# A hybrid gating/state-space layer on one core: mixing in halves, later root transposes, stores on ScalarE's queue, shared border splits, finer side pieces, residual sums in a row

## The chip, the cores and the metric

The kernel runs on one core of a Trainium2 chip. The metric is the device time of one execution in microseconds (us); for several runs, their median. Engines: TensorE (PE), VectorE (DVE), ScalarE (ACT), GpSimd (POOL) and SyncE (SP), which computes nothing here and issues DMAs.

## The reference

One layer over 2048 tokens of width 1024, all in float32. Cut to what is computed:

```python
hc = _rms(ctx) * norm1_w * (1 + csc1) + csh1        # 256 context tokens: only their final scan states are used
_, st_f, st_b = _token_mixer(hc, zero_state, zero_state, ...)
hl = _rms(x) * norm1_w * (1 + sc1) + sh1            # shifts, scales and gates from silu(c) @ w_ada
# _token_mixer(hl, st_f, st_b):
proj = h @ w_in                                     # u, v (1024 each), z (1024), xBC (1536), dt (32)
xbc = silu(conv_centred(xBC))                       # 5 taps
y = ssd_forward + ssd_backward                      # chunks of 128, 16 heads of 64, state 128, 2 groups
g = (y + xs * d_skip) * silu(z)
ssd_out = _rms(g in 2 groups of 512) * ssd_norm_w
u, v = gelu(u), _rms(gelu(v) in 8 heads of 128) * gm_norm_w
mixed = einsum('hts,bcshd->bcthd', gm_ws, v) + gm_bs   # 128 x 128 per head and chunk
x = x + g1 * (concat[u * mixed, ssd_out] @ w_out)
hl = _rms(x) * norm2_w * (1 + sc2) + sh2
x = x + g2 * ((silu(hl @ w_gate) * (hl @ w_up)) @ w2)  # hidden width 2816
return _rms(x) * final_norm_w
```

## The kernel before

Tokens are worked in two blocks of 1024 (blk 1 first, then 0), each in two halves of 512 (TB); a chunk is 128 tokens (P). Every float32 operand of a large product is split in a high and a low part (`hi`, `lo`), and a product of 128 x 128 by 512 columns is done as three (`mm3`, L234 to L236; L1142 to L1144 and L1271 to L1273 in the FFN). ScalarE casts the high part and VectorE subtracts for the low one (`split`, L1026 to L1028; `wlo`, L221, for projection weights). A block of 24 such products fills one of PSUM's banks: 3 are called `mmp`, 5 `smp`.

The stages in order: projection, convolution and transposes of xBC of block 1; `proj_v`, `proj_u`, `proj_z` of block 1 beside context scans and the backward scan; xBC of block 0; then the long stretch of some 800 us in which `run` advances a main chain (`proj_z(0)`, `proj_v(0)`, `proj_u(0)` and three quarters of the output projection, `out_half`) and a side chain in turn: the rest of the backward scan (`ssd_bwd`) and then `ssd_y`, 2.61 side steps (`SIDE`) to each block of main. Then the last quarter of `out_half` with `border`, which prepares the FFN; `ffn1(0)`, `ffn2(0)` (with `prep_1`, the preparation of block 1, as its side), `ffn1(1)`, `ffn2(1)`. The FFN works with seven products of sums for eight (tiles of such sums are made by L1031 and L1034).

`proj_v(blk)`: for two groups of four heads (hh) and two token halves (j), four chunks c: a block of 24 products, gelu (`gelu2`, L588 to L592: square, product, tanh, product), squares for the norm. `mixing(hh, j, vh)` does the four heads' 128 x 128 products (L631) for the j before, when c is 2: for each head it loads weights and biases `gw` (L627, L628; two buffers), multiplies, and adds on VectorE (L633). The last j's mixing stands at the end of `proj_v`. `proj_u` loads the mixed rows (L612) and multiplies them with its gelu.

`ssd_y` walks 32 items (chunk c, group g): `y_load` loads the item's record; `y_seg` (item ahead) loads per half of the heads (q) the factor rows fb and bb from `fscr` (L751, L752), broadcast over all partitions, and makes the masked decay matrices from them (L757 on ScalarE, L758 to L760, L761, product on GpSimd L762); `y_out` does the item's products (L776 to L787), and VectorE's sums (L782 to L798); `y_store` transposes the item's result (L806), copies it and stores it (L809). After every eighth item `y_rstd` computes the reciprocal roots of the group norm with `newton` (L242 to L247: a chain of small VectorE instructions), transposes them (L819), copies and stores them (L822, `r3scr`). Main and side share the pools `tma` (14 buffers), `xin` (8) and `sml`.

What sets the order: the program's calls fix a data flow, and a scheduler that the framework runs ahead of time places the instructions; on the chip each engine takes its own in that fixed order, and an instruction that waits holds all behind it. All DMAs, loads and stores, are issued by SyncE in one such order. In `to_tok` (L471) transposed rows of xBC are stored the same way.

In the FFN, `hl_split` (L1097) splits four tiles of sums, `slow(prep_1(), 2, 10)` puts a piece of the side (four in all) after every ten steps of `ffn2`, `upd` (L1252) adds a finished down product to the residual, `sq_acc` (square on ScalarE L261, add L264) sums its squares, and `final` (L1291: a product with ones, root, L1295 scale, L1296 store) ends a half.

Of the kernel before, what the change touches and what calls it, by code (L numbers as in the profile page):

```python
# [14 lines left out]
P = 128  # L15
# [68 lines left out]
def kernel(ctx: ExitStack, tc: tile.TileContext, xT, ctxp, cc, crow, wad1, wad2, vecs, rows,  # L84
# [378 lines left out]
    def to_tok(o, n, q, ch):  # L463
# [7 lines left out]
        DMA.dma_start(rec[q][g][:, :, coff:coff + P].rearrange("c p x -> p c x"),  # L471
# [132 lines left out]

    def proj_u(blk, hs):
        for h0 in range(0, 8, 2):
            us = [unit(U_U + h0), unit(U_U + h0 + 1)]
            for j in range(2):
                ts_ = slice((blk * 2 + j) * TB, (blk * 2 + j + 1) * TB)
                for i, (hi, lo) in enumerate(us):  # L610
# [4 lines left out]
                    flush()  # L615
                    t = gelu2(ps, tmp)
# [4 lines left out]
    def proj_v(blk, hs):  # L621
        def mixing(hh, j, vh):
            ts_ = slice((blk * 2 + j) * TB, (blk * 2 + j + 1) * TB)
            for h in range(4):
# [3 lines left out]
                DMA.dma_start(gw[:, 1, :], gmb[:, hd * P:(hd + 1) * P].broadcast_to([P, P]))  # L628
                ps = smp()
# [9 lines left out]
        for hh in range(2):  # L639
            us = [unit(U_V + hh * 4 + i) for i in range(4)]  # L640
            for j in range(2):
                vh = []
                ms = sml()[:, :16]
                for c in range(4):
# [8 lines left out]
                    if c == 2 and prev is not None:  # L653
                        mixing(*prev)
# [9 lines left out]
        mixing(*prev)  # L664
# [72 lines left out]

    def y_load(pools, i, c, g):
        return {"rc": load_rec(pools[i % 3 == 2], c, g, True)}

    def y_seg(st, c, g):
# [5 lines left out]
        for q in range(2):  # L747
            h0 = g * 8 + q * 4
            fb, bb = tma()[:, :TB], tma()[:, :TB]
            o = ((c % 4) * 32 + h0) * P  # L750
            DMA.dma_start(fb, fscr[c // 4][:, o:o + TB].broadcast_to([P, TB]))  # L751
            DMA.dma_start(bb, fscr[c // 4][:, o + 16 * P:o + 16 * P + TB].broadcast_to([P, TB]))  # L752
# [50 lines left out]
    def y_store(ya, c, g):  # L803
# [5 lines left out]
        DMA.dma_start(sscr[c // 4][g * TB:(g + 1) * TB, (c % 4) * P:(c % 4 + 1) * P].rearrange("(i p) t -> p i t", p=P),  # L809
# [3 lines left out]
    def y_rstd(tb, ms):  # L813

        V.tensor_scalar(out=ms, in0=ms, scalar1=1.0 / TB, scalar2=4 * EPS, op0=ALU.mult, op1=ALU.add)
        r = newton(ms, 8)
        yield
        ps = smp()
        PE.transpose(out=ps[0:8, :P], in_=r, identity=ident)  # L819
        t = tma()  # L820
        S.copy(t[0:8, :P], ps[0:8, :P])
        DMA.dma_start(r3scr[tb].rearrange("g (c x) -> (g c) x", x=P), t[0:8, :P])  # L822

    def ssd_y(rp):
        its = [(c, g) for c in range(NCH) for g in range(2)]
        st = {}
        st[0] = y_load(rp, 0, *its[0])
        yield from y_seg(st[0], *its[0])
        st[1] = y_load(rp, 1, *its[1])
        store = None  # L830
        for i, (c, g) in enumerate(its):
# [6 lines left out]
            y = yield from y_out(st.pop(i), c, g, ms[:, g * 4 + c % 4:g * 4 + c % 4 + 1])  # L838
            if store is not None:
                yield from y_store(*store)  # L840
            store = (y, c, g)
            if g == 1 and c % 4 == 3:
                yield from y_rstd(c // 4, ms)
        yield from y_store(*store)

# [574 lines left out]
```

## Time and profile before

| what | value |
|---|---|
| runs shown | 2985.91, 2975.28, 2970.30 us (median 2975.28) |
| the profiled execution's own time | 2980.2 us |
| its span, first to last instruction | 2978.4 us |
| mean granted TensorE clock | 0.971 |
| busy: PE, DVE, ACT, POOL | 95%, 66%, 43%, 21% |
| TensorE in the stretch 800 to 1550 us | busy 684.97 of 750, clock 0.95 |

The profile is of one execution. It is read in this order: the busy shares tell which engine has no room; the waits of that engine tell what its gaps are for, each named by its line and by what ended the gap; a timeline of the engine that was late tells why. The granted clock is read beside them, since TensorE works the same product in 0.23 us or 0.43 us by it.

### The profile page before, as it was taken

The page shows a single profiled execution, that of the slowest core. Times are in us where ns is not written, and L with a number is a line of the kernel's source. Part 1 is how long each engine was busy: PE and PEld are TensorE (multiplying, and loading weights), DVE is VectorE, ACT ScalarE, POOL GpSimd, SP SyncE. Part 2 cuts the span into 40 slices and gives each one's busy share as a digit, 9 for nine tenths or more (in the row PEclk, how much of TensorE's full clock was granted, in tenths as well). Part 3 has the DMA queues.
Part 4 walks back from the last instruction along what each step waited for, and adds up shares of the span by engine and source line. Part 5 has one row for each costly group of instructions (what it writes and reads, how often), then busy time and mean ns, then how long its engine had stood idle before and what let it go on. Part 6 is the DMA issues. An engine that isn't in the chain of part 4 may idle for free. (4 is left out here: it accounts for less than half of the span.)

```text
span 2978.4 us, 36719 instructions
## 1 busy us (share of the span) xinstructions
PE 2815.9 (95%) x12478; PEld 2252.8 (76%) x12478; DVE 1977.8 (66%) x3012; ACT 1272.8 (43%) x2360; POOL 637.6 (21%) x550
## 2 busy tenths in 40 slices
PE   7999989999998898998979899999999899999997
PEld 2788778788677676776768688888778788888885
DVE  6776866886678788777876655556766544445555
ACT  4445343344356455443543533333544333333443
POOL 3100000101132232322302344444210322221000
PEclk8999999999999999998989899999999999999998
DMA  6222567742755588786758444445766333334664
GB/s 223 91 88 89 178 217 236 247 135 85 229 178 147 173 248 250 221 257 214 245 164 278 165 152 163 159 151 181 253 218 204 127 106 106 106 100 132 227 192 155
DMA packets 296744, 528.03 MB, mean 177 GB/s; under 512 B 28998, under 2 KB 89830, under 8 KB 296556
## 3 DMA queue, kind: packets, MB, share of 16 engines
q1 hardware_dynamic: 296556, 525.69, 55.3%
q8 instruction: 98, 1.61, 0.2%
q14 instruction: 90, 0.74, 0.1%
HBM read 382.94 MB, written 142.64 MB: 176 GB/s over the span
## 5 line engine op out<-in xcount | busy, mean ns | idle before, releaser
L1028 DVE TENSOR_TENSOR hl<-w,hl 128x1024 fp32r<-128x1024 f32 x286 | 373.5, 1312 | 317.0 <-ACT hl L1027 133.4
L1027 ACT CAST hl<-w 128x1024 fp32r<-128x1024 f32 x286 | 299.0, 1049 | 442.6 <-PE smp L1273 167.8
L234 PE MATMUL mmp<-actt,whi 128*128 128x512 f32 x1120 | 456.1, 407 | 24.9 <-DVE tma L592 15.4
L236 PE MATMUL mmp<-actt,wlo 128*128 128x512 f32 x1120 | 444.3, 397 | 0.0
L235 PE MATMUL mmp<-actt,whi 128*128 128x512 f32 x1120 | 443.1, 396 | 0.2 <-DVE actt L861 0.2
L1144 PE MATMUL mmp<-hl,hl 128*128 128x512 f32 x704 | 277.4, 394 | 9.3 <-DVE hl L1028 9.3
L1142 PE MATMUL mmp<-hl,hl 128*128 128x512 f32 x704 | 277.9, 395 | 7.8 <-ACT t L1167 3.5
L1143 PE MATMUL mmp<-hl,hl 128*128 128x512 f32 x704 | 277.4, 394 | 0.0
L234 PEld LDWEIGHTS mmp<-actt,whi 128*128 128x128 f32 x1120 | 214.6, 192 | 74.9 <-DVE tma L592 17.6
L235 PEld LDWEIGHTS mmp<-actt,whi 128*128 128x128 f32 x1120 | 214.8, 192 | 47.3 <-issue 4.3
L236 PEld LDWEIGHTS mmp<-actt,wlo 128*128 128x128 f32 x1120 | 214.1, 191 | 46.2 <-issue 0.5
L234 PE MATMUL mmp<-whi,actt 128*128 128x512 f32 x512 | 211.1, 412 | 2.4 <-DVE tma L679 2.4
L1142 PE MATMUL smp<-hl,hl 128*128 128x512 f32 x528 | 208.6, 395 | 0.0
L1143 PE MATMUL smp<-hl,hl 128*128 128x512 f32 x528 | 207.3, 393 | 0.0
L235 PE MATMUL mmp<-wlo,actt 128*128 128x512 f32 x512 | 206.8, 404 | 0.0
L236 PE MATMUL mmp<-whi,actt 128*128 128x512 f32 x512 | 206.8, 404 | 0.0
L1144 PE MATMUL smp<-hl,hl 128*128 128x512 f32 x528 | 206.7, 392 | 0.0
L1034 DVE TENSOR_TENSOR t<-smp,t 128x512 f32<-128x512 f32 x88 | 60.4, 687 | 181.6 <-PE smp L1144 132.5
L1034 POOL TENSOR_TENSOR w<-w 128x512 f32<-128x512 f32 x44 | 59.0, 1341 | 486.9 <-DVE hl L1028 320.9
L1144 PEld LDWEIGHTS mmp<-hl,hl 128*128 128x128 f32 x704 | 133.7, 190 | 38.9 <-DVE hl L1028 10.2
L1142 PEld LDWEIGHTS mmp<-hl,hl 128*128 128x128 f32 x704 | 133.5, 190 | 38.4 <-ACT t L1167 4.2
L456 DVE SCALAR_TENSOR_TENSOR tma<-xin,cw,tma 128x512 f32<-128x512 f32 x192 | 144.2, 751 | 21.9 <-ACT tma L454 16.3
(275 smaller groups left out, 5755.5 us busy)
## 6 DMA issues: line engine op xcount, KB each, us to landing
w<-in_wall_dram SPq DMA_DIRECT2D x110, 512.0 KB, 4.0
ws<-in_wall_dram SPq DMA_DIRECT2D x104, 512.0 KB, 3.8
ascr<-t SPq DMA_DIRECT2D x154, 256.0 KB, 3.8
w<-ascr SPq DMA_DIRECT2D x154, 256.0 KB, 3.7
tma<-fscr SPq DMA_DIRECT2D x128, 256.0 KB, 6.2
w<-wscr SPq DMA_DIRECT2D x88, 256.0 KB, 3.1
t<-x2scr SPq DMA_DIRECT2D x76, 256.0 KB, 4.3
w<-in_wall_dram SPq DMA_DIRECT2D x66, 256.0 KB, 3.0
```

The source lines that it names most:

```text
L234: PE.matmul(ps, lhsT=lh, rhs=rh, start=(i == 0), stop=False)
L235: PE.matmul(ps, lhsT=lh, rhs=rl, start=False, stop=False)
L236: PE.matmul(ps, lhsT=ll, rhs=rh, start=False, stop=(i == n - 1))
L456: V.scalar_tensor_tensor(out=acc[:, :n], in0=raw[:, j:j + n], scalar=cw[:, ch, j:j + 1], in1=acc[:, :n], op0=ALU.mult, op1=ALU.add)
L1027: S.copy(hi, x)
L1028: eng.tensor_tensor(out=lo, in0=x, in1=hi.bitcast(F32), op=ALU.subtract)
L1034: eng.tensor_tensor(out=o, in0=a, in1=b, op=ALU.add)
L1142: PE.matmul(ps, lhsT=hi[:, ms_], rhs=t[:, 0, :], start=first and k == 0, stop=False, skip_group_check=not first)
L1143: PE.matmul(ps, lhsT=hi[:, ms_], rhs=t[:, 1, :], start=False, stop=False, skip_group_check=not first)
L1144: PE.matmul(ps, lhsT=lo[:, ms_], rhs=t[:, 0, :], start=False, stop=k == 3, skip_group_check=not first)
```

## The change

Seven edits:

- `to_tok`, `y_store` and the root rows issue their stores (50, 32 and 4) on ScalarE's own queue (`S.dma_start`), behind ScalarE's copy, and no longer on SyncE's.
- `proj_v`: the gate loads are taken out of `mixing` (`gate_load`, for a pair of heads), and `mixing` does a pair at a time: the loads of the first pair at c = 1, its mixing and the second pair's loads at c = 2, the second mixing at c = 3. For the last j both go to the list `tails`, which `proj_u` takes from behind its first blocks.
- `ssd_y`: the factor rows are loaded ahead (`f_load`): those of q = 0 after `y_out` of the item two before, those of q = 1 when q = 0 starts.
- `y_rstd` returns the transposes of the roots as a function, called behind the next item's `y_store`.
- `hl_split` gives the fourth subtraction (k = 3) to GpSimd.
- `ffn2`: all four `upd` stand ahead of the four `sq_acc`; `final(blk, 1)` comes three steps later.
- `prep_1` gives way after each of its 12 pieces, where it did so after every third, and `slow` puts one after every 4 steps of `ffn2`, not 10.

```diff
@@ to_tok, y_store, y_rstd: stores
-        DMA.dma_start(rec[q][g][:, :, coff:coff + P].rearrange("c p x -> p c x"),
+        S.dma_start(rec[q][g][:, :, coff:coff + P].rearrange("c p x -> p c x"),
...
-        DMA.dma_start(sscr[c // 4][g * TB:(g + 1) * TB, (c % 4) * P:(c % 4 + 1) * P].rearrange("(i p) t -> p i t", p=P),
+        S.dma_start(sscr[c // 4][g * TB:(g + 1) * TB, (c % 4) * P:(c % 4 + 1) * P].rearrange("(i p) t -> p i t", p=P),
@@ proj_u
                     flush()
+                    if tails and (j or i):
+                        tails.pop(0)()
                     t = gelu2(ps, tmp)
@@ proj_v
-        def mixing(hh, j, vh):
+        gws = []
+
+        def gate_load(hh, h0):
+            for h in range(h0, h0 + 2):
                 hd = hh * 4 + h
                 gw = sp.tile([P, 2, P], F32, name="gw", tag="gw", bufs=2)
...
+                gws.append(gw)
+
+        def mixing(hh, j, vh, h0):
+            ts_ = slice((blk * 2 + j) * TB, (blk * 2 + j + 1) * TB)
+            for h in range(h0, h0 + 2):
+                hd = hh * 4 + h
+                gw = gws.pop(0)
                 ps = smp()
...
-                    if c == 2 and prev is not None:
-                        mixing(*prev)
+                    if prev is not None:
+                        if c == 1:
+                            gate_load(prev[0], 0)
+                        if c >= 2:
+                            mixing(*prev, 2 * c - 4)
+                        if c == 2:
+                            gate_load(prev[0], 2)
...
-        mixing(*prev)
+        gate_load(prev[0], 0)
+        tails.append(lambda: (mixing(*prev, 0), gate_load(prev[0], 2)))
+        tails.append(lambda: mixing(*prev, 2))
@@ y_seg
+    def f_load(c, g, q):
+        fb, bb = tma()[:, :TB], tma()[:, :TB]
+        o = ((c % 4) * 32 + g * 8 + q * 4) * P
+        DMA.dma_start(fb, fscr[c // 4][:, o:o + TB].broadcast_to([P, TB]))
+        DMA.dma_start(bb, fscr[c // 4][:, o + 16 * P:o + 16 * P + TB].broadcast_to([P, TB]))
+        return fb, bb
...
-            fb, bb = tma()[:, :TB], tma()[:, :TB]
-            o = ((c % 4) * 32 + h0) * P
-            DMA.dma_start(fb, fscr[c // 4][:, o:o + TB].broadcast_to([P, TB]))
-            DMA.dma_start(bb, fscr[c // 4][:, o + 16 * P:o + 16 * P + TB].broadcast_to([P, TB]))
+            fb, bb = st["f"].pop(0)
+            if q == 0:
+                st["f"].append(f_load(c, g, 1))
@@ y_rstd, ssd_y
-        yield
-        ps = smp()
-        PE.transpose(out=ps[0:8, :P], in_=r, identity=ident)
-        t = tma()
-        S.copy(t[0:8, :P], ps[0:8, :P])
-        DMA.dma_start(r3scr[tb].rearrange("g (c x) -> (g c) x", x=P), t[0:8, :P])
+
+        def rows():
+            ps = smp()
+            PE.transpose(out=ps[0:8, :P], in_=r, identity=ident)
+            t = tma()
+            S.copy(t[0:8, :P], ps[0:8, :P])
+            S.dma_start(r3scr[tb].rearrange("g (c x) -> (g c) x", x=P), t[0:8, :P])
+
+        return rows
...
             y = yield from y_out(st.pop(i), c, g, ms[:, g * 4 + c % 4:g * 4 + c % 4 + 1])
+            if i + 2 < len(its):
+                st[i + 2]["f"] = [f_load(*its[i + 2], 0)]
             if store is not None:
                 yield from y_store(*store)
+                if rows is not None:
+                    rows()
+                    rows = None
...
-                yield from y_rstd(c // 4, ms)
+                rows = y_rstd(c // 4, ms)
+                yield
         yield from y_store(*store)
+        rows()
@@ hl_split
-            split(xs[k], hl[p, k][:, 0, :], hl[p, k][:, 1, :])
+            split(xs[k], hl[p, k][:, 0, :], hl[p, k][:, 1, :], (V, G)[k == 3])
@@ ffn2
+        due = None
...
                 for m in range(4):
                     upd(p, m)
+                for m in range(4):
                     j, mm = {2: (0, m), 7: (1, 4 + m), 3: (1, m), 4: (0, 4 + m)}.get(p, (None, None))
...
                 if p == 3:
-                    final(blk, 1, x2, acc[1])
+                    due = n + 3
...
+            if n == due:
+                final(blk, 1, x2, acc[1])
@@ prep_1
-        for i in prep_hl(1, STR_P):
-            if i:
-                yield
+        yield from prep_hl(1, STR_P)
...
-    ffn2(0, slow(prep_1(), 2, 10))
+    ffn2(0, slow(prep_1(), 2, 4))
```

The scheduler's order moves with it. On TensorE, at the first of the four transposes of root rows (L819 before, L845 after; `smp<-ident,sml`): before, it stands inside a block of projection products (`mmp`).

```order
L234 MATMUL mmp_8469<-whi_7337,actt_4652 128x512
L235 MATMUL mmp_8469<-wlo_7338,actt_4652 128x512
L819 MATMUL smp_8412<-ident_232,sml_8364 8x128
L236 MATMUL mmp_8469<-whi_7337,actt_4652 128x512
L234 MATMUL mmp_8469<-whi_7343,actt_4658 128x512
```

After (`gw`: a gating product; `ident,tma`: a y transpose; `h01`, `hb` and `rec_sb`: products of the next item):

```order
L643 MATMUL smp_8594<-gw_8522,xin_8247 128x128
L831 MATMUL smp_8627<-ident_232,tma_8302 128x128 x4
L845 MATMUL smp_8635<-ident_232,sml_8368 8x128
L801 MATMUL smp_8695<-h01_2607,rec_sb_8172 128x512
L802 MATMUL smp_8696<-hb_8424,rec_sb_8172 128x512
```

The root transpose moved from place 3643 to place 3714 on TensorE, directly behind the y transposes of the next item; the second and third moved by 37 and 78 places, the fourth from 5334 to 5333.

On SyncE, in the middle of the long stretch (factor rows `tma<-fscr`, the gated rows for the output projection `xin<-gmscr`, a weight `ws`), before:

```order
L752 DMA tma_9696<-fscr1_101 128x512
L853 DMA xin_9499<-gmscr0_144 128x512
L217 DMA ws_10199<-in_wall_dram 128x1024
L853 DMA xin_9504<-gmscr1_145 128x512
L853 DMA xin_9509<-gmscr2_146 128x512
L853 DMA xin_9514<-gmscr3_147 128x512
L853 DMA xin_9519<-gmscr4_148 128x512
L853 DMA xin_9524<-gmscr5_149 128x512
L853 DMA xin_9529<-gmscr6_150 128x512
L853 DMA xin_9534<-gmscr7_151 128x512
L751 DMA tma_9718<-fscr1_101 128x512
L752 DMA tma_9719<-fscr1_101 128x512
```

The first row is the second of q = 0's pair (fb stands just ahead of it); the last two are the pair of q = 1. After:

```order
L760 DMA tma_9637<-fscr1_101 128x512
L761 DMA tma_9638<-fscr1_101 128x512
L614 DMA tma_9661<-mscr6_142 128x512
L730 DMA rec_sb_9695<-rec20_94 128x1024
L584 DMA gmscr5_149<-tma_9619 128x512
L771 DMA hb_9697<-hscr7_111 128x512
L760 DMA tma_9699<-fscr1_101 128x512
L761 DMA tma_9700<-fscr1_101 128x512
L217 DMA ws_10194<-in_wall_dram 128x1024
L890 DMA xin_9499<-gmscr0_144 128x512
L890 DMA xin_9504<-gmscr1_145 128x512
L890 DMA xin_9509<-gmscr2_146 128x512
```

The pair of q = 0 is now asked for first, ahead of the next record (`rec_sb`) and of `hb`, and the pair of q = 1 stands ahead of the eight loads of `gmscr` instead of behind them.

On VectorE, in the border to the FFN (`hl<-w` is the low part of a weight, `hl_k<-t` that of one of the four tiles of sums), the nine rows up to and with the awaited weight `hl_14115`, before:

```order
L1028 TENSOR_TENSOR hl_2_14007<-t_14051,hl_2_14007 128x512
L1028 TENSOR_TENSOR hl_14083<-t_14032,hl_14083 128x512
L1028 TENSOR_TENSOR hl_3_14008<-t_14053,hl_3_14008 128x512
L1028 TENSOR_TENSOR hl_0_14009<-t_14067,hl_0_14009 128x512
L1028 TENSOR_TENSOR hl_1_14010<-t_14069,hl_1_14010 128x512
L1028 TENSOR_TENSOR hl_2_14011<-t_14071,hl_2_14011 128x512
L1028 TENSOR_TENSOR hl_3_14012<-t_14073,hl_3_14012 128x512
L1028 TENSOR_TENSOR hl_0_14013<-t_14086,hl_0_14013 128x512
L1028 TENSOR_TENSOR hl_14115<-w_13910,hl_14114 128x1024
```

After, from the first split of a tile of sums:

```order
L1065 TENSOR_TENSOR hl_0_13997<-t_13914,hl_0_13997 128x512
L1065 TENSOR_TENSOR hl_1_13998<-t_13916,hl_1_13998 128x512
L1065 TENSOR_TENSOR hl_2_13999<-t_13918,hl_2_13999 128x512
L1065 TENSOR_TENSOR hl_14064<-w_13875,hl_14063 128x1024
L1065 TENSOR_TENSOR hl_0_14001<-t_14024,hl_0_14001 128x512
L1065 TENSOR_TENSOR hl_1_14002<-t_14026,hl_1_14002 128x512
L1065 TENSOR_TENSOR hl_2_14003<-t_14028,hl_2_14003 128x512
L1065 TENSOR_TENSOR hl_14083<-t_14032,hl_14083 128x512
L1065 TENSOR_TENSOR hl_0_14005<-t_14047,hl_0_14005 128x512
L1065 TENSOR_TENSOR hl_14115<-w_13910,hl_14114 128x1024
```

`hl_14115` stood behind 18 small splits and one large; it now stands behind 8 small ones and the same large one, and the `hl_3` of every tile of sums are on GpSimd.

Elsewhere in the order: at the end of the first `ffn2`, SyncE's loads of `x2scr` for the last updates stand ahead of the weight load behind which three of them stood before; in `ffn2(0)` VectorE's splits of the next block alternate with those of the weights.

## Rows read from the trace of the kernel before

**Rows 1.** The page's first part: busy time of the four computing engines, its share of the span, and instructions.

```profile
PE 2815.9 (95%) x12478; PEld 2252.8 (76%) x12478; DVE 1977.8 (66%) x3012; ACT 1272.8 (43%) x2360; POOL 637.6 (21%) x550
```

**Rows 2.** The view of waits, TensorE: operation and line, what it waited for, us in total, times, longest.

```profile
PE smp L819 <- DVE sml L247: 22.9, 4, 8.3
PE mmp L234 <- DVE tma L592: 15.4, 4, 8.0
PE smp L631 <- DMA gw<-in_gmw_dram: 13.7, 8, 6.2
PE smp L1291 <- DVE t L264: 11.9, 2, 6.3
PE mmp L1144 <- DVE hl L1028: 9.3, 2, 8.2
...
PE mmp L1272 <- DVE hl L1028: 5.0, 2, 2.5
...
PE smp L779 <- POOL tma L762: 4.1, 2, 2.9
PE smp L1272 <- DVE hl L1028: 3.5, 2, 2.1
...
PE smp L776 <- DVE tma L782: 2.8, 1, 2.8
...
PE mmp L1142 <- DVE t L1252: 2.3, 1, 2.3
```

**Rows 3.** The timeline of TensorE at the third and the fourth of the small transposes of root rows: start, duration (us), engine, line, operation, count, and in brackets the idle time before it and what ended it. Between the first and the third row shown stand twelve more products like them, each 0.43 us after the one before.

```profile
1351.78 0.37 PE L819 MATMUL smp<-ident,sml 128*8 128x128 f32 x1 [8.27 <-DVE sml L247]
1351.81 0.78 PE L234 MATMUL mmp<-actt,whi 128*128 128x512 f32 x1
...
1357.49 0.39 PE L235 MATMUL mmp<-actt,whi 128*128 128x512 f32 x1
1357.72 0.40 PE L236 MATMUL mmp<-actt,wlo 128*128 128x512 f32 x1
...
1522.64 0.37 PE L819 MATMUL smp<-ident,sml 128*8 128x128 f32 x1 [3.46 <-DVE sml L247]
```

**Rows 4.** The view of stretches, 800 to 1550 us: length, busy time (and instructions) of TensorE, of its weight loads, of VectorE, ScalarE and GpSimd, the granted clock, the DMA share and GB/s.

```profile
800.00:1550.00 750.00, 684.97 (x3099) 538.66 (x3097) 576.50 (x1142) 379.52 (x997) 197.50 (x155) 0.95 0.70 213
```

**Rows 5.** The timeline of SyncE, the queue of all loads and stores, before the longest wait for gate weights (6.18 us, ended at 930.17).

```profile
911.68 0.42 SPq L752 DMA_DIRECT2D tma<-fscr  x1
926.83 0.32 SPq L745 DMA_DIRECT2D hb<-hscr  x1
928.09 0.33 SPq L627 DMA_DIRECT2D gw<-in_gmw_dram  x1
```

**Rows 6.** The timeline of SyncE before the wait of 7.97 us that ended at 1149.03.

```profile
1134.21 4.54 SPq L853 DMA_DIRECT2D xin<-gmscr  x7
1138.80 0.60 SPq L751 DMA_DIRECT2D tma<-fscr  x1
```

**Rows 7.** The timeline of ScalarE at the same place.

```profile
1146.45 1.28 ACT L757 ACTIVATE tma<-tma,nacs 128x128 f32<-128x128 f32 x4 [3.90 <-DMA tma<-fscr]
1147.64 0.61 ACT L591 ACTIVATE tma<-tma 128x512 f32<-128x512 f32 x1
```

**Rows 8.** The view of waits, all engines: ScalarE's first operation on the factor rows.

```profile
ACT tma L757 <- DMA tma<-fscr: 117.9, 44, 6.8
```

**Rows 9.** The timeline of VectorE in the border to the FFN.

```profile
1643.84 4.90 DVE L1028 TENSOR_TENSOR hl<-t,hl 128x512 fp32r<-128x512 f32 x8
...
1649.79 10.43 DVE L1028 TENSOR_TENSOR hl<-t,hl 128x512 fp32r<-128x512 f32 x10
1660.14 1.21 DVE L1028 TENSOR_TENSOR hl<-w,hl 128x1024 fp32r<-128x1024 f32 x1
```

**Rows 10.** The timeline of GpSimd there and a little later.

```profile
1650.00 1.60 POOL L1034 TENSOR_TENSOR w<-w 128x512 f32<-128x512 f32 x1 [13.73 <-ACT hl L1027]
...
1669.32 1.29 POOL L1034 TENSOR_TENSOR w<-w 128x512 f32<-128x512 f32 x1 [12.66 <-DVE hl L1028]
```

**Rows 11.** The timeline of SyncE at the end of the first FFN block.

```profile
2302.25 0.34 SPq L1104 DMA_DIRECT2D w<-in_wall_dram  x1
2311.60 0.33 SPq L1103 DMA_DIRECT2D w<-in_wall_dram  x1
2311.98 1.37 SPq L1250 DMA_DIRECT2D t<-x2scr  x3
```

**Rows 12.** The timeline of VectorE there.

```profile
2316.24 0.75 DVE L1252 SCALAR_TENSOR_TENSOR t<-mmp,m_sb,t 128x512 f32<-128x512 f32 x1 [1.63 <-DMA t<-x2scr]
```

**Rows 13.** The timeline of VectorE at the very end.

```profile
2954.40 0.75 DVE L1252 SCALAR_TENSOR_TENSOR t<-mmp,m_sb,t 128x512 f32<-128x512 f32 x1 [4.66 <-PE mmp L1273]
2955.85 0.69 DVE L264 TENSOR_TENSOR t<-t,t 128x512 f32<-128x512 f32 x1 [0.70 <-ACT t L261]
2956.45 0.75 DVE L1252 SCALAR_TENSOR_TENSOR t<-mmp,m_sb,t 128x512 f32<-128x512 f32 x1
```

**Rows 14.** The view of one line, L809: SyncE's issues of the y stores (minimum, median and longest duration in ns, first and last start).

```profile
L809 SPq DMA_DIRECT2D sscr<-tma x32: 370/371/463, 844.6 to 1524.6; - x32
```

**Rows 15.** The page's last part, DMA issues: count, KB each, median us from issue to landing.

```profile
tma<-fscr SPq DMA_DIRECT2D x128, 256.0 KB, 6.2
...
gw<-in_gmw_dram SPq DMA_DIRECT2D x32, 64.0 KB, 4.7
```

More of the change, by code (lines that the diff above doesn't have):

```diff
@@ L603, in stat_terms @@
         return r
+    tails = []
     def proj_u(blk, hs):
@@ L621, in proj_v @@
     def proj_v(blk, hs):
-        def mixing(hh, j, vh):
-            ts_ = slice((blk * 2 + j) * TB, (blk * 2 + j + 1) * TB)
-            for h in range(4):
+        gws = []
+        def gate_load(hh, h0):
+            for h in range(h0, h0 + 2):
                 hd = hh * 4 + h
@@ L827, in ssd_y @@
         st[0] = y_load(rp, 0, *its[0])
+        st[0]["f"] = [f_load(*its[0], 0)]
         yield from y_seg(st[0], *its[0])
         st[1] = y_load(rp, 1, *its[1])
-        store = None
+        st[1]["f"] = [f_load(*its[1], 0)]
+        store = rows = None
         for i, (c, g) in enumerate(its):
```

## The prediction

> **What bounds the kernel now.** First the busy shares [rows 1]: TensorE works 2815.9 us of the span of 2978.4, VectorE 66%, so TensorE sets the time, and only its gaps (162 us with the start) and its slow stretches can be won; no product is taken away. Next the view of TensorE's waits [rows 2]: which operation stood, for whom. The ten rows sum to 90.9 us, and in all but the gate row the releaser is another engine that came late, VectorE mostly. Then the timeline around one such wait [rows 3]: the wait at 1351.78 took 8.27 us, and behind it 13 products started in 5.68 us (1351.81 to 1357.49), where the next step, 1357.49 to 1357.72, is 0.23 us: the clock is at its lower level (1.2 GHz) after the pause. A long wait so costs 5.68 - 13 x 0.23 = 2.7 us more. Last the stretch 800 to 1550 us [rows 4], where projections and scan outputs run side by side: TensorE busy 685 of 750, VectorE 576.5 (77%), clock 0.95. No second engine is full, but VectorE isn't far.
>
> **The change part by part.** Gains are against the profiled execution, 2980.2 us; "bound" is the most that can go.
>
> *Root transposes.* Four waits, 22.9 us [rows 2]; the fourth is 3.46 [rows 3], and the order leaves its place as it was, so 19.4 is open. In the other three the transpose moves behind the y transposes of the next item, 37 to 78 of TensorE's instructions later. The newton chain that TensorE awaits is then long done. Bound 19.4 + 3 x 2.7 = 27.5. VectorE was late there, though, and evicts TensorE's three mmp banks: part of its lag will show at the next eviction. At 77% load it catches up within a few blocks, but not at once; I take two thirds, 18.
>
> *Gates.* 13.7 us in 8 waits [rows 2]. The queue row shows why [rows 5]: SyncE stood from 912.1 to 926.83 before a load of hb whose buffer VectorE still used, and only then issued the gate load of the second heads (928.09). Its landing takes 4.7 us [rows 15]. Now the first pair is asked for one block earlier (24 x 0.23 = 5.5 us) and the second at the first mixing, one block before its use. 5.5 against 4.7 is little, and the queue can still stand. Bound 13.7 + 2.7 = 16.4, low 0; I take 11, since the stores that waited in that queue for ScalarE have gone to ScalarE's own.
>
> *Factor rows.* At 1149.03 TensorE waited 8.0 us for a gelu's L592 [rows 2]: SyncE issued seven loads of gmscr (4.54 us) ahead of the factor rows [rows 6], ScalarE stood 3.90 us for them at L757 with the gelu's tanh (L591) behind it [rows 7], VectorE's L592 behind that. This is one of 44 such stops, 117.9 us [rows 8]; most are hidden, and I lay the 4.1 and 2.8 us of L779 and L776 [rows 2] to them too. The order after has the same pair ahead of the gmscr loads. Bound 8.0 + 4.1 + 2.8 + 2 x 2.7 = 20.3; low, with the buffers that the early rows hold, -8; I take 12.
>
> *Last mixing behind the first blocks of proj_u.* The L592 row has 15.4 - 8.0 = 7.4 us left in three waits [rows 2], shorter ones where proj_u starts behind proj_v's newton and mixing. Bound 7.4; I take 3, since the same VectorE work comes two blocks later.
>
> *Border.* TensorE waited 8.2 us for one split of VectorE (L1144) [rows 2], which stood behind 18 small ones [rows 9]: 8 in 4.90 us (0.61 each), then 10 in 10.43 (1.04 each) while GpSimd was at work, whose own subtraction took 1.60 us beside them and 1.29 later [rows 10]. Now five small splits go to GpSimd, and the awaited one stands behind 8 small and 1 large. From 1643.84 it would end after 8 x 0.61 + 2 x 1.21 = 7.3 us alone (1651.1), or after 8 x 1.04 + 2 x 1.21 x 1.04 / 0.61 = 12.4 us beside GpSimd (1656.3); it ended at 1661.35 before. So 5.0 to 10.2 us earlier, of 8.2 that count; with the clock, bound 10.9. GpSimd's five last 5 x 1.29 to 1.60 = 6.5 to 8 us, which can slow VectorE for 5 us more; low -6; I take 5. The Trainium skill speaks against this part: "GPSIMD Engine Reference", section 1 "Specifications", has GpSimd share its SBUF interfaces with VectorE, with contention where VectorE reads two SBUF inputs. The 1.04 against 0.61 agrees; by the rule alone this part would give 0, and the sum 52 where the rows' way gives 57.
>
> *Side pieces in the down projection.* L1272's two rows, 8.5 us in four waits [rows 2]: VectorE met the next block's splits in a bunch. Now they alternate with the weights' splits. Bound 8.5; I take 5 (the first wait is not of these).
>
> *End of the first FFN block.* L1142 waited 2.3 us for an update and L1291 11.9 - 6.3 = 5.6 us for the sum [rows 2]. SyncE stood from 2302.6 to 2311.60 at a weight load ahead of three loads of x2scr [rows 11], and VectorE's update came at 2316.24 [rows 12]. After the change these loads stand ahead of that weight, the four updates ahead of the sums, and the sum's product three steps later. Bound 7.9 + 2.7 = 10.6; I take 8.
>
> *Tail.* Update 0.75, square, add, four times 2.05 (2954.40 to 2956.45) [rows 13], so the last add ends at 2962.7. In a row the updates end near 2957.2, and four adds follow 0.6 apart: about 2959.7. 3 us, bounds 2 to 3.4.
>
> *ScalarE's own stores.* 86 issues leave SyncE. On SyncE one takes 0.37 us [rows 14]; ScalarE issues no DMA in this trace, so each costs it 0 to 0.46, 0 to 40 us in all. It is busy 379.5 of 750 us in the scan stretch [rows 4] and 43% overall [rows 1], so most is covered by idle time; the 36 in the y chain lie ahead of activations for which gelus wait. I take 4 lost, and 4 more for waits on tma buffers.
>
> Sum: 18 + 11 + 12 + 3 + 5 + 5 + 8 + 3 - 8 = 57; 2980.2 - 57 = 2923. The profiled run lies 4.9 us above the median of the runs (2975.3), so a median would be 2918. All bounds together are 105 us: 2870.
>
> **The rivals.**
> (a) *The side chain sets the pace from 800 to 1550.* If TensorE only meets VectorE's lag one eviction later, roots, gates and factor rows give nothing, and the rest is 3 + 5 + 5 + 8 + 3 = 24: 2951. For it: most releasers are VectorE. Against: 77%, and 173 us in which it is idle itself.
> (b) *Slower: the early rows starve the tma pool.* It has 14 buffers; each early pair takes two from main blocks, so a gelu waits for one, and TensorE for a bank. The price is that of a row which comes late, its landing, 6.2 us [rows 15]. At 32 items, it turns the sum over if more than 65 / 6.2, about 10 items, pay it; half of them: 16 x 6.2 - 65 = +34: 3009. Against: only one pair is ahead, and for about one step.
> (c) *GpSimd's splits slow VectorE through the border.* Nothing of 8.2 is won and 6 are lost: 57 - 11 = 46, 2929. Rows 9 speak for it, the new place of the awaited split against; the page named above has this rule.
> (d) *It doesn't do what it says with the gates:* two gw buffers allow the second pair only after the first mixing's last read, and landing plus queue outlast a block: 57 - 11, also 2929.
> (e) *Nothing:* the stalls move on everywhere; 2965 to 2980.
>
> **How the numbers follow.** Forecast (2895 to 2940) 0.52, (c) and (d) 0.05 each, (a) 0.20, spread 2940 to 2965, (e) 0.10, (b) 0.08. Predicted 2918. The low end 2878 leaves out only sums within 8 us of all bounds; the high end 2963 takes in (a), and leaves out (b) and (e), 0.18. Half a per cent, 15 us, is about what a measurement of this kernel tells from no change: 2960.4 and 2990.2. Faster: 0.52 + 0.10 + 0.19 = 0.81; slower: 0.07 of (b); same 0.12.
>
> **What would show it.** Right: L845 has three waits near zero and one of 3 to 4 us; the gate row falls below 4; no wait at L592 over 4 us; ScalarE's wait for fscr well below 117.9; TensorE's wait in the border below 5; the last add near 2.4 us after the updates' end; the clock of 800 to 1550 above 0.95. Wrong: a new large row of TensorE waiting on VectorE's evictions in the scan stretch with VectorE over 85% busy there (a); SyncE or ScalarE standing for tma buffers (b); border splits beside GpSimd over 1.04 us and TensorE still waiting 8 us (c); ScalarE's issues far over 0.46 us each.

## The result and the profile after

| kernel | median of its runs, us | lowest and highest |
|---|---|---|
| before (4 runs) | 2974.7 | 2970.3 to 2985.9 |
| changed (4 runs) | 2927.3 | 2922.0 to 2932.3 |

The ratio is 0.9837 with a 95% interval of 0.9807 to 0.9866: 47 us less by the medians, where 57 was forecast. The profiled execution of the changed kernel took 2923.6 us (span 2921.8), 57 less than that of before. The changed kernel timed a second time gave 2922.8 (0.981, 0.9782 to 0.9838).

TensorE's busy row, beside [rows 1]:

```profile
PE 2803.1 (96%) x12478; PEld 2242.7 (77%) x12478; DVE 1975.6 (68%) x3007; ACT 1274.2 (44%) x2361; POOL 645.4 (22%) x555
```

Its busy time fell by 13 us with no product taken away: that is clock (the mean granted one rose from 0.971 to 0.980). The rest of the 57 are gaps. Its waits, beside [rows 2], with the operation, what it waited for, us in total, times, longest:

```profile
PE smp L1332 <- DVE t L264: 9.6, 2, 5.8
...
PE smp L643 <- DMA gw<-in_gmw_dram: 6.2, 4, 2.4
PE smp L845 <- DVE tma L807: 5.2, 2, 4.3
PE smp L802 <- DVE tma L807: 5.2, 1, 5.2
...
PE smp L801 <- issue: 4.6, 1, 4.6
...
PE mmp L234 <- DVE tma L592: 4.6, 3, 3.2
PE smp L831 <- DVE tma L823: 3.8, 1, 3.8
...
PE smp L831 <- DVE tma L807: 2.6, 2, 2.3
...
PE smp L1310 <- DVE hl L1065: 1.1, 2, 0.6
...
PE smp L845 <- DVE sml L247: 0.7, 1, 0.7
```

The roots' row (L845) has fallen from 22.9 to 5.9 us in its two rows, the gates (L643) from 13.7 to 6.2, L592 from 15.4 to 4.6, the down projection's splits (L1310) from 8.5 to 1.1. Other waits of the same stretch have grown: on VectorE's L807 and L823 at L802 and L831, and one at L801 for which the view names no releaser, 16.2 us in all. L801 and L802 are the products that stood at L776 and L777 before, where they waited 6.2 us (2.8, 2.0 and 1.4). The final sum (L1332) still waits 9.6.

To see where time went, the program is cut at landmarks on TensorE, read from its timeline: the first state product of block 1, the first transpose of block 0's xBC, the first state product of block 0, the first FFN product, the first product of the first down projection, the end. Stage lengths in us, one profiled execution each; the last row is the range over the kernels below whose change doesn't touch that stage, which is the size of chance.

| | start | projections, block 1 | xBC, block 0 | scan stretch | border and first up projection | rest |
|---|---|---|---|---|---|---|
| before | 285.5 | 326.0 | 143.5 | 885.1 | 444.8 | 893.5 |
| changed | 288.3 | 310.3 | 145.2 | 863.2 | 439.4 | 875.5 |
| untouched, range | 287.9 to 290.1 | 310.3 to 315.0 | 144.1 to 149.3 | 856.5 to 863.2 | 437.6 to 441.6 | 872.8 to 876.1 |

The stretch 800 to 1550 us, beside [rows 4]:

```profile
800.00:1550.00 750.00, 701.14 (x3172) 552.22 (x3172) 592.20 (x1160) 388.46 (x1004) 202.80 (x155) 0.96 0.70 217
```

TensorE is busy 701 of 750 instead of 685, VectorE 592 (79%), the clock 0.96.

### The profile page after: what moved, and what is told of

It reads as the page before. It is cut to its first block, busy times and chain, and to the rows that moved or that the text cites. A ratio compares the mean times of both kernels' runs of the same rounds, so it can differ in the third digit from the quotient of the medians.

```text
span 2921.8 us, 36695 instructions
## 1 busy us (share of the span) xinstructions
PE 2803.1 (96%) x12478; PEld 2242.7 (77%) x12478; DVE 1975.6 (68%) x3007; ACT 1274.2 (44%) x2361; POOL 645.4 (22%) x555
## 5 line engine op out<-in xcount | busy, mean ns | idle before, releaser
L787 POOL TENSOR_TENSOR tma<-tma 128x512 f32<-128x512 f32 x64 | 93.4, 1461 | 339.4 <-ACT tma L786 138.4
L1179 PEld LDWEIGHTS mmp<-hl,hl 128*128 128x128 f32 x704 | 132.7, 189 | 32.5 <-ACT t L1204 3.0
```

The lines of the kernel that those rows point to most:

```text
L1179: PE.matmul(ps, lhsT=hi[:, ms_], rhs=t[:, 0, :], start=first and k == 0, stop=False, skip_group_check=not first)
```

## The experiments

Two theories run through them. Theory 1, that of the prediction: each wait is local, so each part, when undone alone, gives its own time back. The rival: in the scan stretch VectorE and the side chain set the pace, so an ended wait comes up again elsewhere. Each kernel is the changed one with one part undone, but for the first (nothing undone) and those of the last two groups. "Mean" is that of the untouched stages: start and xBC together 434.5, projections 311.5, scan stretch 860.7, border 439.8, rest 874.6.

### The changed kernel again

> The changed kernel once more, for the size of chance differences. Stage lengths in its first trace: projections of block 1 (first scan-state product to the first transpose of block 0's xBC) 310.3 us, scan stretch (first state product of block 0 to the first FFN product) 863.2, border and first up projection 439.3, first down projection 212.8. Expected of every theory: each stage within 2 us of these, the scan stretch within 4, the ratio to the kernel before between 0.981 and 0.987.

2922.8 us; stages 288.6, 311.1, 145.5, 862.8, 440.7 and 875.2. Two executions of one kernel agree within 1.3 us a stage; but of kernels that share the order of the scan stretch, three took 856.5 to 860.4, so 4 us there prove nothing. TensorE's gate row differs too, between executions of one kernel: 8.8 us here, 6.2 above.

### Stores on SyncE

```diff
-        S.dma_start(sscr[c // 4]...      (so too rec in to_tok, r3scr in rows)
+        DMA.dma_start(sscr[c // 4]...
```

> The 86 stores back on SyncE, all else as changed. Theory 1 (each part of the change ends its own wait, and ScalarE's issues cost about what SyncE's queue gains): the time within 8 us of the changed kernel, TensorE's wait for gate weights between 6 and 10 us. Theory 2 (the stores that left SyncE's queue carry the gain of gates and factor rows): 15 us or more slower, the gate row back at 12 or more. A third (ScalarE's issues are a loss): 5 us or more faster.

2914.1 us, 0.9783 (0.9760 to 0.9806): 9 below the changed kernel timed beside it, with intervals that overlap. The stages tell more: start 286.2 and xBC 142.9, below all untouched ones (together 5.4 under the mean), and the scan stretch 856.2, 4.5 under the mean and at the edge of chance. So the third theory is the nearest: ScalarE's stores are a loss, of some 5 us in the start and xBC, and some 9 in all by the medians. Whether the issues on ScalarE or the later landings (below) make the loss was not told apart. Theory 1 had the gate row between 6 and 10; it is 2.9 (first row), so the relief of SyncE's queue isn't what shortened it. An issue costs ScalarE what it cost SyncE [rows 14], and the stores land later, beside SyncE's 3.0 us before: the line's view and the DMA issues of the changed kernel (median us to landing last):

```profile
PE smp L643 <- DMA gw<-in_gmw_dram: 2.9, 3, 2.1
```

```profile
L834 ACTq DMA_DIRECT2D sscr<-tma x32: 366/366/431, 831.6 to 1491.6; - x32
```

```profile
sscr<-tma ACTq DMA_DIRECT2D x32, 256.0 KB, 6.1
```

The Trainium skill, "DMA: Bandwidth & Descriptors", section "Rules for kernel authors", has it that spreading DMAs over issuing engines saves only the sequencer's issue time. These runs agree: the 0.37 us that SyncE saved on each store were paid on ScalarE, in front of its activations, and the time got no shorter.

### Mixing whole

```diff
-                        if c == 1:
-                            gate_load(prev[0], 0)
-                        if c >= 2:
-                            mixing(*prev, 2 * c - 4)
-                        if c == 2:
-                            gate_load(prev[0], 2)
+                        if c == 2:
+                            for h0 in (0, 2):
+                                gate_load(prev[0], h0)
+                                mixing(*prev, h0)
```

> All four heads' gate loads and mixing at the third chunk again (the last mixing of a block still goes behind the first blocks of proj_u). Theory 1: TensorE's gate row from 6.2 back to 11 to 14 us, the scan stretch 7 to 10 us longer, projections of block 1 unchanged within 3. Theory 2 (the queue, not the halves): the gate row below 8 and every stage within 2 us.

2936.0 us. The gate row is back, and more:

```profile
PE smp L643 <- DMA gw<-in_gmw_dram: 16.6, 8, 4.9
```

The scan stretch took 869.4 (8.7 over the mean), as theory 1 said, but the projections of block 1 took 317.8, 6.3 over: the halves help there too, which it had not said. In that stage the changed kernel's rows have no gate wait; here there are five:

```profile
PE smp L643 <- DMA gw<-in_gmw_dram: 4.3, 5, 1.7
```

### The last mixing at the end of proj_v

```diff
-        gate_load(prev[0], 0)
-        tails.append(lambda: (mixing(*prev, 0), gate_load(prev[0], 2)))
-        tails.append(lambda: mixing(*prev, 2))
+        for h0 in (0, 2):
+            gate_load(prev[0], h0)
+            mixing(*prev, h0)
```

> Halves kept, but the last mixing of a block stands at the end of proj_v again. Theory 1: the three waits of 2 to 3 us where proj_u starts (L592 twice, the gating product once) come back with their clock, projections of block 1 9 to 15 us longer (310.3 to about 322), the scan stretch 0 to 5 longer. Theory 2 (the gain of that stage comes from the halves): that stage within 4 us.

2934.1 us; projections 320.2 (8.7 over the mean), scan stretch 864.1 (3.4 over the mean, 0.9 beyond the untouched range, which proves nothing). The waits of proj_u are back:

```profile
PE mmp L234 <- DVE tma L592: 13.0, 6, 4.2
```

In the projections of block 1 they are two, of 4.2 and 2.8 us, and behind each six or seven products follow 0.43 us apart; the gating product waits 1.4 us.

### Factor rows late

```diff
-            fb, bb = st["f"].pop(0)
-            if q == 0:
-                st["f"].append(f_load(c, g, 1))
+            fb, bb = f_load(c, g, q)
```

(and the two earlier calls of `f_load` gone)

> Factor rows loaded where they are used again, all else as changed. Theory 1 (each part ends its own waits): ScalarE's wait for fscr from 85.8 us back to 110 or more, the scan stretch 8 to 16 us longer (863 to 871 to 879). Theory 2 (the stretch goes at the pace of VectorE and the side chain; a wait that is ended comes up again elsewhere): ScalarE's wait rises too, but the stretch stays within 4 us. A third (the early rows hold buffers and cost): 3 us or more shorter.

2937.4 us, 0.9881 (0.9865 to 0.9896). The scan stretch took 877.3, 16.6 over the mean and 14.1 over the changed kernel, the upper end of theory 1. But ScalarE's wait for fscr rose only from 85.8 to 93.8, where 110 was said; what rose are a few long waits of TensorE:

```profile
ACT tma L782 <- DMA tma<-fscr: 85.8, 39, 5.9
```

```profile
ACT tma L780 <- DMA tma<-fscr: 93.8, 37, 6.5
```

```profile
PE smp L810 <- DVE h L812: 12.6, 1, 12.6
...
PE smp L800 <- DVE tma L805: 8.8, 1, 8.8
PE mmp L234 <- DVE tma L592: 8.2, 2, 7.2
```

The wait of 8.8 stands behind the rows: ScalarE's L780 waited for them, with VectorE's L781 and L805 behind it. The wait of 12.6, ended by L812 at 1387.2, does not: VectorE, which had no gap over 1.02 us from 1362.84 on, came to L812 only after eight multiplications for the output projection (L889).

```profile
1480.94 1.28 ACT L780 ACTIVATE tma<-tma,nacs 128x128 f32<-128x128 f32 x4 [2.76 <-DMA tma<-fscr]
```

```profile
1381.16 5.47 DVE L889 SCALAR_TENSOR_TENSOR xin<-xin,vec,tma 128x512 f32<-128x512 f32 x8 [1.02 <-issue]
1386.55 0.68 DVE L812 TENSOR_TENSOR h<-h,smp 128x512 f32<-128x512 f32 x1
```

So the total of ScalarE's wait is no measure of its price (with the stores on SyncE it was 112.3 in a faster kernel); which few of the stops reach TensorE is. And part of the 16.6 is the order, which shifts with the loads, and not a late row; how large a part is not known. The third theory, that held buffers cost, falls.

### Roots early

```diff
-                rows = y_rstd(c // 4, ms)
-                yield
+                yield from y_rstd(c // 4, ms)     # which yields once, then transposes, copies and stores
```

> The root transposes directly behind their newton chain again. Theory 1: three waits of 5 to 8 us on L247 come back, the scan stretch 12 to 22 us longer. Theory 2: the waits come back, while those on L807, L823 and L814 (19 us in the changed kernel) shrink by as much; the stretch 0 to 6 us longer.

2927.3 us, 0.9847 (0.9830 to 0.9864).

```profile
PE smp L846 <- DVE sml L247: 23.0, 3, 9.9
...
PE smp L831 <- DVE tma L807: 2.1, 2, 1.9
PE smp L802 <- DVE tma L807: 1.2, 1, 1.2
```

All 23.0 us are back, in three waits, but the scan stretch is 872.4, 11.7 over the mean and 9.2 over the changed kernel: between the theories. The wait on L247 is 22.3 us longer than in the changed kernel (23.0 against 0.7). Of that, 9.7 are spared on L807: its waits at L845, L802 and L831 are 13.0 us in the changed kernel's rows above and 3.3 here. So the later transposes moved some two fifths of the wait to VectorE's next eviction. The waits on L823 (3.8 there, 4.1 here) are the same in both and no part of it. By the ratios the whole kernel is 3 to 11 us slower than the changed one.

### All border splits on VectorE

```diff
-            split(xs[k], hl[p, k][:, 0, :], hl[p, k][:, 1, :], (V, G)[k == 3])
+            split(xs[k], hl[p, k][:, 0, :], hl[p, k][:, 1, :])
```

> All small border splits on VectorE again. Theory 1 (the gain is the new place of the awaited split): if the order puts that split early here too, the border is within 3 us of the changed kernel; if it goes back behind 18 small ones, the 8 us wait comes back, 5 to 9 us. Theory 2 (the work taken off VectorE is the gain): 3 to 6 us longer in either order. Theory 3 (contention makes sharing a loss): 2 us or more shorter.

The order puts the awaited split behind 18 small ones again. The border stage took 445.5, 5.7 over the mean and beyond the range, and a wait of 5.0 us is back. The total, 2925.0, doesn't tell it; in the profiled execution the scan stretch, where nothing differs, was the shortest of all untouched ones (856.5).

```profile
PE mmp L1181 <- DVE hl L1065: 6.7, 2, 5.0
```

It is 5.0 and not 8.2 us as in the kernel before, because here VectorE's ten splits took 0.6 us each, and one subtraction of GpSimd's beside them took 9.96 us; before, the two slowed each other (see *Border* below). VectorE's rows, then GpSimd's:

```profile
1612.22 6.10 DVE L1065 TENSOR_TENSOR hl<-t,hl 128x512 fp32r<-128x512 f32 x10
```

```profile
1612.44 9.96 POOL L1071 TENSOR_TENSOR w<-w 128x512 f32<-128x512 f32 x1 [13.76 <-ACT hl L1064]
```

Theory 1's case; theory 3 (sharing is a loss) falls. Theory 2 isn't told apart, since place and work went together.

### Side pieces ten steps apart

```diff
-    ffn2(0, slow(prep_1(), 2, 4))
+    ffn2(0, slow(prep_1(), 2, 10))          # and prep_1 gives way at every third piece
```

> Side pieces of the first down projection as before (four, ten steps apart). Theory 1: TensorE's waits of 1.4 to 2.5 us on the splits come back, the first down projection 7 to 12 us longer (212.8 to 220 to 225), nothing else changes. Rival (the sums in a row carried that stage's 14.7 us): within 3 us.

2939.0 us, 0.9884 (0.9866 to 0.9902); the first down projection 224.5 instead of 212.7, the rest of the FFN as it was. The stage in both, by stretches (length, busy time of TensorE, its weight loads, VectorE, ScalarE, GpSimd, then the granted clock), first here, then in the changed kernel:

```profile
2049.60:2274.10 224.50, 215.33 (x927) 175.60 (x926) 159.87 (x175) 115.30 (x139) 33.37 (x16) 0.98 0.68 227
```

```profile
2046.30:2259.00 212.70, 211.57 (x927) 173.32 (x925) 162.43 (x175) 114.48 (x138) 30.16 (x15) 1.00 0.72 240
```

Of 11.8 us, 8.0 are gaps and 3.8 are products at the lower clock: a wait of 2.42 us was followed by products 0.43 us apart, and so was one of 2.54. The longest, 3.05 us, was not:

```profile
2136.74 0.80 PE L1310 MATMUL mmp<-hl,hl 128*128 128x512 f32 x1 [2.42 <-DVE hl L1065]
2137.33 0.63 PE L1311 MATMUL mmp<-hl,hl 128*128 128x512 f32 x1
2137.76 0.63 PE L1309 MATMUL mmp<-hl 128*128 128x512 f32 x1
...
2158.38 0.50 PE L1310 MATMUL smp<-hl,hl 128*128 128x512 f32 x1 [3.05 <-DVE hl L1065]
2158.71 0.39 PE L1311 MATMUL smp<-hl,hl 128*128 128x512 f32 x1
2158.94 0.40 PE L1310 MATMUL smp<-hl,hl 128*128 128x512 f32 x1
```

### Updates and sums in turn, the sum's product early

```diff
                 for m in range(4):
                     upd(p, m)
-                for m in range(4):
...
-                    due = n + 3
+                    final(blk, 1, x2, acc[1])
```

> Updates and sums of squares in turn again, and the sum of the other half's product at its first place. Theory 1: the end of the last down projection 2 to 3.5 us longer; the first down projection 3 to 8 us longer, with the update's wait of 2.3 us back. Rival (that stage's gain is the side pieces' alone): the first down projection within 2 us.

2929.6 us. The last stage is 2.5 longer (232.5 instead of 230.0), as said. At the end of the first down projection the update's wait of 2.3 us is back, but down and up projection together are only 1.3 longer (646.8 instead of 645.5): the forecast's 8 us are not there.

### The last half's sum later still

```diff
                 if p == 4:
-                    final(blk, 0, x2, acc[0])
+                    if blk == 0:
+                        fin.append(lambda: final(blk, 0, x2, acc[0]))
+                    else:
+                        final(blk, 0, x2, acc[0])
...
                 stage_y(t)                      # in ffn1
+            if fin and t == 0:
+                fin.pop()()
```

> A version beyond the change: in block 0 the sum's product of the last half (L1332, which still waited 5.8 us) is called behind the first stage of the second up projection. Theory (the wait is only for VectorE's sums, 9 us behind the last product, which 36 products of 0.23 us now cover): that wait falls below 1 us, 5 to 8 us with the clock. Rival (the eight residual tiles held longer starve the up projection's temporaries): the wait moves to them, within 2 us or slower.

2914.3 us, 0.9790 (0.9772 to 0.9808). The second up projection took 424.2 instead of 432.8; of the two waits for the final sums one is left, that at the very end. Why it stood before, in the changed kernel, first TensorE's row, then VectorE's:

```profile
2261.70 0.40 PE L1181 MATMUL mmp<-hl,hl 128*128 128x512 f32 x1
2267.88 2.08 PE L1332 MATMUL smp<-t,ones 128*128 128x512 f32 x2 [5.78 <-DVE t L264]
```

```profile
2258.16 2.06 DVE L1289 SCALAR_TENSOR_TENSOR t<-mmp,m_sb,t 128x512 f32<-128x512 f32 x3
2260.14 0.74 DVE L1289 SCALAR_TENSOR_TENSOR t<-smp,m_sb,t 128x512 f32<-128x512 f32 x1
2260.80 0.68 DVE L264 TENSOR_TENSOR t<-t,t 128x512 f32<-128x512 f32 x1
2261.40 2.30 DVE L1065 TENSOR_TENSOR hl<-w,hl 128x1024 fp32r<-128x1024 f32 x1
2263.62 4.21 DVE L264 TENSOR_TENSOR t<-t,t 128x512 f32<-128x512 f32 x3
```

The updates do come early now, but a weight split (2.30 us) stands among the adds, and the last three adds take 4.21 us, the first of them 1.74 beside GpSimd's work; all of it ends 9 us behind the last down product (2258.6), and only 12 products of the next stage, 2.9 us, stand ahead of the waiting one.

### Stores and sums together, and the stores alone on the kernel before

The first is the changed kernel with both edits above (stores on SyncE, last sum later); the second the kernel before with only its 86 stores moved to `S.dma_start`.

> The changed kernel with its 86 stores back on SyncE and the last sum's product of the first down projection called behind the first stage of the next up projection. Theory (both edits end separate losses): the scan stretch near 857 us, the second up projection near 424, about 2902 us, ratio to the kernel before 0.973 to 0.977. Rival (the lower time with the stores on SyncE was chance in the scan stretch, whose length varies from 856 to 863 us in profiles of kernels that share its order): about 2912, ratio 0.979.

2909.5 us, 0.9772 (0.9755 to 0.9789), the fastest of all. Its profiled execution has the scan stretch at 853.1 and the up projection at 424.2; start and xBC together 426.8, 5.1 below the kernel with the later sum alone. That execution is the fastest of the four (2901.3). By the ratio the kernel lies between the two cases, nearer the first, by the time nearer the second (2912), and the interval all but spans both; the gain of the stores alone stays uncertain in size, about 5 to 10 us.

> The kernel before with only its 86 stores moved to ScalarE's queue. Theory 1 (an issue costs ScalarE 0.37 us in which gelus and evictions stand behind it, which the relief of SyncE's queue doesn't pay): 4 to 12 us slower, the first and the second transposing stage 2 us longer each. Theory 2 (with late gate loads and late factor rows SyncE's queue is the bottleneck, and its relief pays): 4 us or more faster, gate row below 10 us.

2978.7 us, 1.0004 (0.9991 to 1.0018), 11 runs against 15: no difference, so neither theory as a whole. Start and xBC together are 3.9 us longer (432.9 instead of 429.0), as theory 1 said of them; the scan stretch, 888.6, and the projections, 323.4, are no farther from before than chance reaches. It may be that SyncE's relief pays here what ScalarE loses, and that in the changed kernel, whose late loads have been moved ahead, there is little left to relieve. That is argued and not shown: the gate row is 12.5 here instead of 13.7, and ScalarE's wait for the factor rows 100.4 instead of 117.9, but the scan stretch is no shorter.

## Why the prediction held, step by step

The bound was read rightly: TensorE's gaps and the clock behind them. The sum came out near (57 forecast, 57 by the profiles, 47 by the medians), its terms less so. The third column is measured by undoing one part, from the stages of one profiled execution, against the mean of untouched stages. The last is a check on it from all executions: the ratio of the kernel with the part undone less that of the changed one (0.9837 and 0.9810), times 2975 us.

| term | forecast | measured, by stages | by the ratios |
|---|---|---|---|
| roots | 18 | 11.7 | 3 to 11 |
| gates in halves | 11 | 15.0 (8.7 scan stretch, 6.3 projections) | 4 to 12 |
| last mixing in proj_u | 3 | 8.7 (and 3.4 unclear) | 4 to 12 |
| factor rows | 12 | 16.6 (part of it order) | 13 to 21 |
| border | 5 | 5.7 | 1 to 9 |
| side pieces | 5 | 11.8 | 14 to 22 |
| end of the first FFN block | 8 | about 1 | 1 to 9 with the tail |
| tail | 3 | 2.5 | |
| ScalarE's stores and buffers | -8 | -5 to -10 (stores) | -8 to -16 |

- *Roots, too large.* The reason given for taking two thirds was right, and its size wrong: VectorE's lag showed again right behind, on L807, and 9.7 of 22.3 us were given back. The fourth transpose, laid at 3.46 as before, waits 0.7. It's as much of rival (a) as there is; (a) itself falls, since in the scan stretch the three parts undone singly cost 8.7 + 16.6 + 11.7 = 37 us. That this is more than the stage gained as a whole (24 against the mean, with the stores' loss of 4.5 in it) says that these parts end partly the same waits.
- *Gates and last mixing, too small.* The working of the gates looked at block 0's waits; undone, they cost 4.3 us of gate waits in block 1 too. That of the last mixing took "shorter ones where proj_u starts", which was right as to place, with a bound of 7.4; the gating product's own wait and the lower clock behind two of the waits were left out.
- *Side pieces, bound broken.* The bound of 8.5 us left out the lower clock, for the working gave that only to long waits. In the kernel before, the waits of 2.54, 2.42 and 2.13 us of this stage were each followed, at once or a few products on, by six or more products 0.43 us apart (that of 1.40 was not), and TensorE was busy 5.1 us longer than in the changed kernel. The stage before:

```profile
2084.90:2312.40 227.50, 216.71 (x928) 176.88 (x926) 161.76 (x175) 115.11 (x138) 34.89 (x16) 0.98 0.67 221
```

- *End of the first FFN block, failed.* The working laid L1291's 5.6 us to updates that came late and counted on "the sum's product three steps later". The change delays only the other half's product; the one that waits stands where it stood, and waits for adds (5.8 us). The kernel with that sum called later moved it, and 8.6 us came in the second up projection.
- *Border.* The awaited split ended 11.5 us after the first small one began; 7.3 to 12.4 was worked out. But 12.4 is no upper bound. Its 1.04 us for a split beside GpSimd is a mean over ten, of which only four met GpSimd's work, from 1650.00 [rows 10] to 1656.66. One by one, a small split beside GpSimd takes 1.7 us, before as after, and 0.6 without it; an estimate by these rows for eight small and two large ones all beside it is 8 x 1.7 + 2 x 2.22 = 18. Three small ones and one large met GpSimd's work: 5 x 0.6 + 3 x 1.7 + 2.22 + 1.21 = 11.5. That no more did is luck. The sign of rival (c), splits over 1.04 us beside GpSimd, came, but the wait of 8 us did not come with it, since the awaited split has fewer ahead: (c) falls. VectorE's rows, beside [rows 9], one split by itself beside GpSimd (the first in the kernel before, with the last of GpSimd's work there, the second in the changed one), and two of GpSimd's in the changed one:

```profile
1610.70 3.00 DVE L1065 TENSOR_TENSOR hl<-t,hl 128x512 fp32r<-128x512 f32 x3
1613.61 2.30 DVE L1065 TENSOR_TENSOR hl<-w,hl 128x1024 fp32r<-128x1024 f32 x1
1615.83 5.28 DVE L1065 TENSOR_TENSOR hl<-t,hl 128x512 fp32r<-128x512 f32 x5
1621.03 1.21 DVE L1065 TENSOR_TENSOR hl<-w,hl 128x1024 fp32r<-128x1024 f32 x1
```

```profile
1650.48 1.67 DVE L1028 TENSOR_TENSOR hl<-t,hl 128x512 fp32r<-128x512 f32 x1
```

```profile
1654.95 1.71 POOL L1031 TENSOR_TENSOR t<-w,w 128x512 f32<-128x512 f32 x1
```

```profile
1616.44 1.78 DVE L1065 TENSOR_TENSOR hl<-t,hl 128x512 fp32r<-128x512 f32 x1
```

```profile
1619.11 1.45 POOL L1065 TENSOR_TENSOR hl<-t,hl 128x512 fp32r<-128x512 f32 x1 [1.45 <-ACT hl L1064]
1621.19 2.22 POOL L1065 TENSOR_TENSOR hl<-t,hl 128x512 fp32r<-128x512 f32 x1 [0.63 <-ACT hl L1064]
```

- *Tail*, as worked out: four updates and four adds, the last ending at 2906.1, 3.0 us behind the updates where 2.4 was said.

```profile
2900.32 2.11 DVE L1289 SCALAR_TENSOR_TENSOR t<-mmp,m_sb,t 128x512 f32<-128x512 f32 x3 [4.62 <-PE mmp L1311]
2902.36 0.75 DVE L1289 SCALAR_TENSOR_TENSOR t<-smp,m_sb,t 128x512 f32<-128x512 f32 x1
2903.03 3.07 DVE L264 TENSOR_TENSOR t<-t,t 128x512 f32<-128x512 f32 x4
```

- *Rival (b)*, early rows that starve the pool, falls with the late rows' kernel; *(d)* falls with the gate row at 6.2, *(e)* with the result.
- *The signs.* Most came: no wait at L592 over 3.2 us, ScalarE's wait for fscr at 85.8, no border wait on VectorE over 2.5, the clock at 0.96. Two did not: the gate row was to fall below 4 and is 6.2 and 8.8 in the two executions of the changed kernel, and L845's one long wait, 4.3 us, is not the fourth and not for the newton chain.

The total held because terms taken too large (roots, end of FFN: 13 us) and too small (gates, mixing, rows, side pieces: 21) lay on both sides, less what parts that end the same waits share. That they balance was not worked out; so near a sum is in part luck.

## What to carry to other kernels

A wait of the bounding engine costs its length, and often the slow clock behind it too, also when it is only 2 us long; put that into the bound for every wait, for which waits bring it isn't told by their length (2.13 us did here, 3.05 did not). Before a gap is credited to an edit, find in the order the very instruction that waits, and see whether the edit moves that one. Moving the 86 stores to ScalarE's queue paid in neither kernel: nothing in the one before, a loss of some 5 to 10 us in the changed one. A rate taken from a merged row of a timeline is a mean; look at the single instructions before it is called the rate beside another engine.

## What the hardware showed that was not expected

A pause of TensorE of 2.42 us was followed by products 0.43 us apart (1.2 GHz) for some 3 us, one of 3.05 us in the same stage by none. An add of VectorE's of 128 x 512 took 1.74 us beside GpSimd's work (at 2263.62) and 0.69 with GpSimd idle; a split of that size 1.7 and 0.6. With all splits on VectorE they kept their 0.6, and GpSimd's subtraction beside them took 9.96 us, where it takes 1.29 alone [rows 10]; why one engine gave way there, and both elsewhere, is open. A store to sscr (256 KB) took 6.1 us to land when ScalarE issued it and 3.0 before, when SyncE did; it is 3.6 in the changed kernel with the stores on SyncE. The stores to rec of the same size show less of it (3.3 from ScalarE, 2.8 with all of them on SyncE). Why was not tried.
